# Offsetting weight tiles and activation tiles of a decoder layer by 0, 16, 32 or 48 bytes within 64

## The chip, the cores and the metric

The kernel runs on one core of a Trainium2 chip. The metric is the device time of one execution in microseconds (us). Of the kernel before, three runs gave 895.13, 894.33 and 894.97 us; the median is 894.97 us. A difference of under 0.2% of that (1.8 us) counts as no change here.

## The reference, cut to what matters

One layer of a hybrid decoder on 512 tokens of 1024 features, in float32. What is left out here are the insides of the three branches.

```python
h = _rmsnorm(x, g_mix)
proj = h @ w_in                      # 1024 x 7424: RG-LRU input and gate, q/k/v, memory q, three branch gates
y_lru, y_dil, y_mem = ...            # RG-LRU scan, dilated attention, memory attention; each @ its own output weight
merged = sum_b sigmoid(gates_b + b_gate_b) * y_b
x = x + merged @ w_out               # 1024 x 1024
hm = _rmsnorm(x, g_mlp)
x = x + jnp.square(jax.nn.relu(hm @ w_mlp_in)) @ w_mlp_out    # 1024 x 4096, 4096 x 1024
return _rmsnorm(x, g_final)
```

## The kernel before, in words

Every large product is made of three: a float32 operand is split into a high part in a shortened float32 form (`whi`, `hT_hi`, `ah`) and the exact remainder in the same form (`wlo`, `hT_lo`, `al`), and the kernel adds high by high, high by low and low by high in PSUM.

Weights come in slabs of 1 MB from DRAM into two `raw` buffers. `split_w` (line 162) makes from each half of a slab a tile `whi` (ScalarE, a copy) and a tile `wlo` (VectorE, a subtraction), both 128 x 1024 numbers, that is 4096 bytes in each partition. Each of the two names has four buffers used in turn.

A matmul on TensorE has a stationary operand, loaded into the array by a weight load (PEld in the profile), and a moving operand that streams through the array column by column. While one matmul streams, the weight load of the next one runs. Two forms matter:

- `mm3` (line 187, matmuls at lines 191 to 193), used for the input projection, the branch outputs and the first MLP product. The weight tile is stationary, the activations move: `hT` (normalised x, transposed), `hmT` (the same for the MLP), `y`, `odh`/`odl`, `omh`/`oml` (branch results) with 512 columns, `mT` (memory) with 256. A weight tile serves 24 matmuls in a row. `half_proj` (lines 247 to 251) does the same in halves of 256 columns.
- `out_step` (line 932, matmuls at lines 936 to 938), used for the output projection and the second MLP product. Here the activations are stationary and the weight tile moves with 512 columns (256 in the last token tile). The activations are `mrg` (eight merged tiles), `ah`/`al` (the first three of eight tiles of each quarter of the MLP) and `act` (the other five). `mrg` and `act` share ten buffers of 4096 bytes. `v_proj` (lines 513 to 515) also lets the weights move, with 256 columns.

The MLP runs in four quarters: `mlp_in(q+1)` is issued ahead of `mlp_out(q)`. The order of all engines' instructions comes out of the tile framework, which also gives every tile its address and every instruction its waits. Its pools place tiles at multiples of 32 bytes. In the built program the tiles of this story lie at these addresses modulo 64 bytes:

| tiles | before | after |
|---|---|---|
| `hT`, `hmT`, `y`, `odh`, `odl`, `omh`, `oml`, `ah`, `al` | 32 | 32 |
| `mT`, LRU inputs and gate weights, memory-attention tiles | 0 | 0 |
| `whi`, four buffers in turn | 32, 32, 32, 32 | 32, 48, 32, 48 |
| `wlo`, four buffers in turn | 32, 32, 32, 32 | 32, 16, 32, 16 |
| `mrg` and `act` in the shared buffers | 0 | 0, 0, 16, 48 and again |
| the fourth of eight activation tiles of a quarter | 0 | 32 |

Every slice that a matmul takes of these tiles begins a multiple of 512 bytes into its tile, so the address modulo 64 is that of the tile. What the text calls the relation of a pair is the address of the stationary operand that is being loaded minus the address of the operand that moves meanwhile, modulo 64. Counted over the built programs, pairs in the shortened float32 form:

| relation | 512 columns, before | after | 256 columns, before | after |
|---|---|---|---|---|
| 0 (equal) | 2516 | 1399 | 529 | 295 |
| 32 apart | 726 | 258 | 125 | 56 |
| 16 | 0 | 963 | 0 | 142 |
| 48 | 0 | 622 | 0 | 161 |

Of the kernel before, what the change touches and what calls it, by code (L numbers as in the profile page):

```python
# [12 lines left out]
F32R = mybir.dt.float32r  # L13
# [4 lines left out]
P = 128  # L18
# [34 lines left out]
def _bucket_onehots():  # L53
    """[33, 3, 384]: column m of group g picks the bias row at its offset; row 32 marks masked offsets."""
    oh = np.zeros((NUM_BUCKETS + 1, 3, 384), np.float32)
    m = np.arange(384)
    for g in range(3):
        if g == 0:
            off = 255 - m
            valid = (off >= 0) & (off <= 128)  # L60
            dist = off
        elif g == 1:
            off = 127 - m
            valid = off >= 0
            dist = 4 * off
        else:
            off = 127 - m
            valid = (off >= 0) & (off % 4 == 0)
            dist = 4 * off
        b = _bucket(np.maximum(dist, 0))  # L70
        for j in m:
            oh[b[j] if valid[j] else NUM_BUCKETS, g, j] = 1.0
    return oh


def _head_select():
    """[4, 2, 128]: column p of pair hp picks head 2*hp + p // 64."""
    s = np.zeros((HPG, 2, P), np.float32)
    for hp in range(2):
        for p in range(P):  # L80
            s[2 * hp + p // HD, hp, p] = 1.0
    return s


class _Engine:
    """An engine whose instructions can be pinned to program order."""

# [15 lines left out]
class _Interleave:  # L103
    """Program order: dense matmul groups advance a clock; side generators yield the delay (in us of
    tensor-engine work) that their next step should stay behind."""

# [33 lines left out]
def hybrid_block(ctx: ExitStack, tc: tile.TileContext, x, mem, g_mix, w_in, b_gate, conv_w, conv_b,  # L140
# [19 lines left out]

# [1 line left out]
    def split_w(src, n1, n2, lo_eng=None):  # L162
        hi = wp.tile([P, n1, n2], F32R, name="whi", tag="whi", bufs=4)
        A.activation(hi, src, AF.Copy)
        lo = wp.tile([P, n1, n2], F32R, name="wlo", tag="wlo", bufs=4)
        (lo_eng or V).tensor_sub(lo, src, f(hi))
        return hi, lo
# [8 lines left out]
    def slab(parts):  # L176
        """parts: (weight, first column) of 128 columns each; yields the split halves one by one."""
        raw = raw_tile(KT, 256)
        if parts[0][0] is parts[1][0] and parts[0][1] + P == parts[1][1]:
            nc.sync.dma_start(raw, cols(parts[0][0], parts[0][1], 256))  # L180
        else:
            for i, (w, c0) in enumerate(parts):
                nc.sync.dma_start(raw[:, :, i * P:(i + 1) * P], cols(w, c0, P))
        return [split_w(raw[:, :, i * P:(i + 1) * P], KT, P) for i in range(len(parts))]

    def mm3(ps, w, act, nk, k0=0, us=0.648):
        """ps = w.T @ act over nk row blocks, w = (hi, lo) stationary, act(k) -> (hi, lo) moving."""
        whi, wlo = w
        for k in range(nk):
            ah, al = act(k)  # L190
            PE.matmul(ps, whi[:, k0 + k, :], ah, start=k == 0, stop=False)  # L191
            PE.matmul(ps, whi[:, k0 + k, :], al, start=False, stop=False)  # L192
            PE.matmul(ps, wlo[:, k0 + k, :], ah, start=False, stop=k == nk - 1)  # L193
            if k % 2 == 1 and k < nk - 1:
                sch.tick(2 * us)
        # the caller ticks the rest after its evacuation

# [1 line left out]
    ident = cst.tile([P, P], F32, name="ident")  # L199
# [7 lines left out]
    def rstd(xt, sq, tag):  # L207
        """sq: scratch as wide as xt; returns [P, 1] rsqrt(mean(x^2) + eps)."""
        ss = sm.tile([P, 1], F32, name="ss", tag="ss" + tag, bufs=2)
        A.activation(sq, xt, AF.Square, accum_out=ss)  # L210
        return rstd_of(ss, tag)
# [12 lines left out]
    def transp(hn, dst, t):  # L224
        """hn [tokens, D] of token tile t, transposed and split into dst = (hi, lo)."""
        for half in range(2):
# [12 lines left out]
    def half_proj(items, act, evac, mid):  # L239
        """items: split stationaries; two token halves, the second after mid() was emitted."""  # L240
        pss = [psum() for _ in items]
# [14 lines left out]

# [1 line left out]
    xr = x.rearrange("o (t p) d -> p (o t) d", p=P)  # L258
# [16 lines left out]
    nc.sync.dma_start(first_raw[:, :, P:256], cols(w_in, O_GELU, P))  # L275
    # the tensor engine's clock gate opens while the first tokens are on their way
    warm = psum()
# [17 lines left out]

    # per-feature vectors, one column per 128 features
    vrow = st.tile([72, P], F32, name="vrow")
# [14 lines left out]

# [1 line left out]
    ylru = {}  # L314
# [31 lines left out]
    def lru_gate(c, xc, xh, xlo, rg_hi, rg_lo):  # L346
# [11 lines left out]
        V.scalar_tensor_tensor(xc, ti, 1.0, xc, op0=ALU.add, op1=ALU.mult)  # L358
        # t = tanh(-log(a) / 2) = (1 - a) / (1 + a); 1 / (1 + t) starts from (1 + a) / 2
        rc = t512("rc", 1)  # L360
# [21 lines left out]
    def start_rest():  # L382
        """the other two token tiles, the constants, then what the first LRU chunk needs."""
        for t in (2, 3):
            transp(hns[t], hT, t)

    def small_consts():
# [5 lines left out]
        for g in range(3):  # L393
            ps = psum()
            PE.matmul(ps[0:HPG, 0:384], rb[:, g * HPG:(g + 1) * HPG], oh[:, g, :], start=True, stop=True)
            V.tensor_copy(bvec[:, g, :], ps[0:HPG, 0:384])
        # Toeplitz bias tiles: 128 copies of each vector, read back with a row pitch one short
        n_ = HPG * 3 * 384
# [14 lines left out]

    # softplus(-lam) = max(-lam, 0) + log1p(exp(-|lam|)), log1p(e) = 2 atanh(e / (2 + e))
    sp2 = cst.tile([P, NC_LRU], F32, name="sp2")
# [50 lines left out]
    softplus()  # L466
    # block-diagonal recurrence gates, two 64-blocks per 128 features
    rg_raw = raw_tile(2 * NC_LRU, P)
# [8 lines left out]
    V.tensor_sub(rg_lo, rg_raw, f(rg_hi))  # L477
# [1 line left out]
    def q2k(name, dt=F32):  # L479
        return big.tile([P, S], dt, name=name, tag="q", bufs=12)  # L480

    def qk_proj(g, nm):
        """two chunks (heads 0-1, 2-3) of q (scaled) or k; groups 1, 2 in residue order (t mod 4, t // 4)."""
        o = (O_Q if nm == "q" else O_K) + g * 256
# [15 lines left out]
    def v_proj(g):  # L500
        """[128 tokens, 4 token tiles, 256]; token tile = block for group 0, residue for groups 1, 2,
        which are brought to residue order on their way through DRAM."""
        vt = big.tile([P, 4, 256], F32, name="vt", tag="V", bufs=4)
# [24 lines left out]

    # memory tokens, normalised here and transposed once there is room
    mr = mem.rearrange("o (t p) d -> p (o t) d", p=P)  # L530
# [31 lines left out]

# [1 line left out]
    mT = (ap_.tile([P, KT, N_MEM], F32R, name="mT_hi", tag="mT_hi"),  # L564
# [7 lines left out]

# [1 line left out]
    def softmax_stats(sc, mz, i):  # L574
        """sc [P, 4 heads, n]: exp(s - max) in place; mz[:, 0|1, i, :] = max, sum."""
        V.tensor_reduce(mz[:, 0, i, :], sc, axis=AX.X, op=ALU.max)
# [10 lines left out]
    def p_T(groups):  # L587
        """groups of 4 [128, 128] slices, transposed; returns SBUF tiles [128 keys, 4, 128 queries]."""
        res = []
# [31 lines left out]
    def av_out(dst, view, terms):  # L621
        """terms: (transposed P [keys, 4, queries], V [keys, 256]) summed into [128, 2 head pairs, 128]."""
        ps = psum()
# [37 lines left out]
    def stats_T(mz, permute):  # L661
        """mz [P tokens, 2, 4 tiles, 4 heads] -> [4 heads, 2, 512 tokens] in token order."""
        st_ = pr_tile([HPG, 2, S], "stT")
# [14 lines left out]
    def side_b():  # L678
# [4 lines left out]
        for r in range(4):  # L683
# [7 lines left out]
            yield 1.0  # L691
        # merge by the softmax denominators
        sA = stats_T(mzA, False)
# [47 lines left out]

# [1 line left out]
    km = []  # L743
# [38 lines left out]

# [1 line left out]
    omem = {}  # L784
# [59 lines left out]

# [1 line left out]
    branches = (ylru, odil, omem)  # L846
# [63 lines left out]
    def act_tile(name):  # L910
        return ep.tile([P, 2, S], F32R, name=name, tag="act", bufs=10)

# [4 lines left out]

# [1 line left out]
    x2 = {}  # L919
# [48 lines left out]

# [1 line left out]
    def hmmov(k):  # L970
        return hmT[0][:, k, :], hmT[1][:, k, :]

    def mlp_evac(act, ps):
# [5 lines left out]
        else:  # L979
            t_ = act_tile("act")  # L980
            ah, al = t_[:, 0], t_[:, 1]
# [95 lines left out]
```

## Time and profile before

| | |
|---|---|
| median of three runs | 894.97 us |
| span of the profiled execution, first to last instruction | 892.8 us |
| TensorE matmul / weight load busy | 879.6 us / 734.8 us |
| VectorE / ScalarE / GpSimd busy | 451.6 / 356.7 / 26.0 us |
| matmul records | 4383 |
| DMA, mean over the span | 106 GB/s |

The profiled execution is one execution, and its own time is known by its span: 892.8 us, 2.2 us under the median of the runs; these 2.2 us lie outside the first and the last instruction. A matmul's record is longer than the distance to the next matmul's start, since matmuls overlap: what one costs in a dense stretch is the distance from start to start, read from the timeline.

### The profile page before, as it was taken

Reading aid. Unit: us, or ns where it says so; the run is one execution under the profiler, and the core shown is the slowest. Engines: PE = TensorE matmul, PEld = TensorE weight load, DVE = VectorE, ACT = ScalarE, POOL = GpSimd, SP = SyncE. Lnnn points to the kernel's source line nnn. Section 1 sums busy time; section 2 is a strip of 40 time slices with the busy share of each in tenths; the row PEclk is TensorE's granted clock in tenths of the full one; section 3 lists DMA queues with packets and bytes.
Section 4 is the critical chain, followed back from the end, with each engine's and each line's share of the span. In section 5 each row is a group of like instructions: output and inputs, shape, how many; then the busy total and the mean of one; then the engine's idle time right before and its main releaser. Section 6 shows DMA issues by size and latency. Waiting matters only on the chain.

```text
span 892.8 us, 10656 instructions
## 1 busy us (share of the span) xinstructions
PE 879.6 (99%) x4383; PEld 734.8 (82%) x4383; DVE 451.6 (51%) x628; ACT 356.7 (40%) x565; POOL 26.0 (3%) x34
## 2 busy tenths in 40 slices
PE   8999999999999999999999999999999999999997
PEld 7788888889888888888888888888888888888886
DVE  5778666764678543343424365444334433443342
ACT  5457666654644532332323154433113311441122
POOL 3110000000000000000000000000000000000020
PEclk9899999999999999999999999999999999999999
DMA  7673333333421222332434214322333323332202
GB/s 239 186 227 95 95 95 95 95 111 127 140 85 60 70 96 71 118 97 81 130 133 160 83 46 144 95 94 96 94 96 97 106 90 97 111 105 93 98 6 94
DMA packets 79164, 94.87 MB, mean 106 GB/s; under 512 B 3611, under 2 KB 64103, under 8 KB 78988
## 3 DMA queue, kind: packets, MB, share of 16 engines
q1 hardware_dynamic: 77916, 88.15, 31.6%
q0 software_dynamic: 1056, 5.52, 1.9%
q8 instruction: 34, 0.56, 0.3%
q10 hardware_dynamic: 144, 0.52, 0.1%
q14 instruction: 14, 0.11, 0.0%
HBM read 91.03 MB, written 5.52 MB: 108 GB/s over the span
## 4 chain that ended last, share of the span: by engine, by line
PE 92%; DVE 2%; DMA 2%; ACT 1%; issue 1%; POOL 0%; SPq 0%; POOLq 0%; ACTq 0%; DVEq 0%
PE ps L191 19%; PE ps L192 19%; PE ps L193 18%; PE ps L938 8%; PE ps L936 8%; PE ps L937 8%; PE ps L513 1%; PE ps L515 1%; PE ps L514 1%; DMA x<-in_x_dram 1%; PE ps L248 1%; PE ps L626 1%; PE ps L247 1%; PE ps L593 1%; PE ps L251 1%
## 5 line engine op out<-in xcount | busy, mean ns | idle before, releaser
L95 DVE TENSOR_TENSOR wlo<-raw,whi 128x1024 fp32r<-128x1024 f32 (+1 forms) x153 | 182.9, 1199 | 314.2 <-ACT whi L95 309.7
L95 ACT ACTIVATE whi<-raw 128x1024 fp32r<-128x1024 f32 (+1 forms) x154 | 159.5, 1037 | 394.2 <-PE ps L192 223.0
L191 PE MATMUL ps<-hT_hi,whi 128*128 128x512 f32 x400 | 156.6, 392 | 0.0
L193 PE MATMUL ps<-hT_hi,wlo 128*128 128x512 f32 x400 | 155.9, 390 | 0.0
L192 PE MATMUL ps<-hT_lo,whi 128*128 128x512 f32 x400 | 155.9, 390 | 0.0
L192 PE MATMUL ps<-hmT_lo,whi 128*128 128x512 f32 x240 | 93.4, 389 | 0.0
L193 PE MATMUL ps<-hmT_hi,wlo 128*128 128x512 f32 x240 | 93.4, 389 | 0.0
L191 PE MATMUL ps<-hmT_hi,whi 128*128 128x512 f32 x240 | 93.2, 389 | 0.0
L191 PEld LDWEIGHTS ps<-hT_hi,whi 128*128 128x128 f32 x400 | 75.1, 188 | 16.4 <-issue 0.6
L193 PEld LDWEIGHTS ps<-hT_hi,wlo 128*128 128x128 f32 x400 | 75.1, 188 | 15.8
L192 PEld LDWEIGHTS ps<-hT_lo,whi 128*128 128x128 f32 x400 | 75.1, 188 | 15.2
L938 PE MATMUL ps<-whi,act 128*128 128x512 f32 (+1 forms) x165 | 64.1, 389 | 0.0
L937 PE MATMUL ps<-wlo,act 128*128 128x512 f32 (+1 forms) x165 | 64.1, 388 | 0.0
L936 PE MATMUL ps<-whi,act 128*128 128x512 f32 (+1 forms) x165 | 64.1, 388 | 0.0
L192 PEld LDWEIGHTS ps<-hmT_lo,whi 128*128 128x128 f32 x240 | 45.1, 188 | 9.3
L191 PEld LDWEIGHTS ps<-hmT_hi,whi 128*128 128x128 f32 x240 | 45.0, 188 | 9.4
L193 PEld LDWEIGHTS ps<-hmT_hi,wlo 128*128 128x128 f32 x240 | 45.1, 188 | 9.3
L95 DVE TENSOR_TENSOR x<-x,ps 128x512 f32<-128x512 f32 (+1 forms) x41 | 27.7, 675 | 24.9 <-PE ps L938 24.6
L938 PE MATMUL ps<-whi,al 128*128 128x512 f32 (+1 forms) x99 | 38.0, 384 | 0.0
L937 PE MATMUL ps<-wlo,ah 128*128 128x512 f32 (+1 forms) x99 | 37.9, 383 | 0.0
L936 PE MATMUL ps<-whi,ah 128*128 128x512 f32 (+1 forms) x99 | 37.9, 383 | 0.0
L937 PEld LDWEIGHTS ps<-wlo,act 128*128 128x128 f32 x165 | 31.0, 188 | 7.1
(253 smaller groups left out, 1355.6 us busy)
## 6 DMA issues: line engine op xcount, KB each, us to landing
raw<-in_w_in_dram SPq DMA_DIRECT2D x23, 1024.0 KB
raw<-in_w_mlp_in_dram SPq DMA_DIRECT2D x16, 1024.0 KB
raw<-in_w_mlp_out_dram SPq DMA_DIRECT2D x16, 1024.0 KB
raw<-in_w_in_dram SPq DMA_DIRECT2D x12, 512.0 KB
raw<-in_w_mem_kv_dram SPq DMA_DIRECT2D x4, 1024.0 KB
raw<-in_w_out_dram SPq DMA_DIRECT2D x4, 1024.0 KB
x<-in_x_dram SPq DMA_DIRECT2D x7, 512.0 KB
raw<-in_w_lru_out_dram SPq DMA_DIRECT2D x4, 768.0 KB
```

The lines of the kernel that those rows point to most:

```text
L95: r = fn(*a, **k)
L191: PE.matmul(ps, whi[:, k0 + k, :], ah, start=k == 0, stop=False)
L192: PE.matmul(ps, whi[:, k0 + k, :], al, start=False, stop=False)
L193: PE.matmul(ps, wlo[:, k0 + k, :], ah, start=False, stop=k == nk - 1)
L247: PE.matmul(ps[:, sl], whi[:, k, :], ah, start=k == 0, stop=False)
L248: PE.matmul(ps[:, sl], whi[:, k, :], al, start=False, stop=False)
L251: PE.matmul(ps[:, sl], wlo[:, k, :], act[0][:, k, sl], start=False, stop=k == KT - 1)
L513: PE.matmul(ps[:, 0:256], ah, hi[:, k % 4, :], start=k == 0, stop=False)
L514: PE.matmul(ps[:, 0:256], ah, lo[:, k % 4, :], start=False, stop=False)
L936: PE.matmul(ps, ah[:, sl], hi[:, k % 2, :], start=k == 0, stop=False)
L937: PE.matmul(ps, ah[:, sl], lo[:, k % 2, :], start=False, stop=False)
L938: PE.matmul(ps, al[:, sl], hi[:, k % 2, :], start=False, stop=k == KT - 1)
```

## The change

The tile pools get new names for the same buffers. Instead of four buffers under one name, `whi` and `wlo` have one buffer under each of four names, used in the same turn; every other one is 16 bytes longer, and the data begins 16 bytes into it. The framework rounds the longer tiles up to 32 bytes, so that the tiles behind them move by 32. The shared activation buffers get the same treatment with four names of two buffers: eight in place of ten. Since a quarter of the MLP needs five and two quarters live at once, the fourth of its eight activation tiles goes to a buffer of another name (`y4`, of which four hold `x2` and two are free by then). Comments and docstrings go too.

```diff
+    turn = {"w": 0, "act": 0}
+
+    def shifted(pool, name, n1, n2, j, bufs):
+
+        o = 4 * (j % 2)
+        t = pool.tile([P, 1024 + o], F32R, name=name, tag=f"{name}{j}", bufs=bufs)
+        return t[:, o:o + n1 * n2].rearrange("p (a b) -> p a b", a=n1)
+
     def split_w(src, n1, n2, lo_eng=None):
-        hi = wp.tile([P, n1, n2], F32R, name="whi", tag="whi", bufs=4)
+        j = turn["w"] % 4
+        turn["w"] += 1
+        hi = shifted(wp, "whi", n1, n2, j, 1)
         A.activation(hi, src, AF.Copy)
-        lo = wp.tile([P, n1, n2], F32R, name="wlo", tag="wlo", bufs=4)
+        lo = shifted(wp, "wlo", n1, n2, j, 1)
         (lo_eng or V).tensor_sub(lo, src, f(hi))
         return hi, lo
...
     def act_tile(name):
-        return ep.tile([P, 2, S], F32R, name=name, tag="act", bufs=10)
+        turn["act"] += 1
+        return shifted(ep, "act", 2, S, turn["act"] % 4, 2)
...
         if i < 3:
             ah, al = q2k("ah", F32R), q2k("al", F32R)
         else:
-            t_ = act_tile("act")
+            t_ = act_tile("act") if i > 3 else big.tile([P, 2, S], F32R, name="act3", tag="y4", bufs=6)
             ah, al = t_[:, 0], t_[:, 1]
```

No instruction is added, removed or moved: on each of the five engines the built program of the changed kernel has the same instructions with the same shapes in the same order, and with the same waits but for one. The load of `gbmlp` (line 237, in the output projection's lead) waits in addition for an earlier DMA of GpSimd's queue, because its buffer now overlaps one that this DMA used.

## Rows read from the trace of the kernel before

**Rows 1.** The page: busy times, granted clock by slices, the chain by engine

```profile
span 892.8 us, 10656 instructions
...
PE 879.6 (99%) x4383; PEld 734.8 (82%) x4383; DVE 451.6 (51%) x628; ACT 356.7 (40%) x565; POOL 26.0 (3%) x34
...
PEclk9899999999999999999999999999999999999999
...
PE 92%; DVE 2%; DMA 2%; ACT 1%; issue 1%; POOL 0%; SPq 0%; POOLq 0%; ACTq 0%; DVEq 0%
```

**Rows 2.** Timeline of TensorE (start us, length us), 55 matmuls of `mm3`, relation equal

```profile
127.69 0.39 PE L193 MATMUL ps<-hT_hi,wlo 128*128 128x512 f32 x1
127.92 0.39 PE L191 MATMUL ps<-hT_hi,whi 128*128 128x512 f32 x1
...
139.93 0.39 PE L193 MATMUL ps<-hT_hi,wlo 128*128 128x512 f32 x1
```

**Rows 3.** Timeline of TensorE, 36 matmuls of `out_step`, relation 32 apart

```profile
631.76 0.40 PE L936 MATMUL ps<-whi,act 128*128 128x512 f32 x1
...
639.93 0.40 PE L938 MATMUL ps<-whi,act 128*128 128x512 f32 x1
```

**Rows 4.** Timeline of TensorE, 77 matmuls of `v_proj`, 256 columns, relation equal

```profile
81.83 0.28 PE L515 MATMUL ps<-whi,hT_lo 128*128 128x256 f32 x1
...
90.94 0.28 PE L513 MATMUL ps<-whi,hT_hi 128*128 128x256 f32 x1
```

**Rows 5.** Timeline of TensorE, 11 matmuls on `mT`, 256 columns, relation 32 apart

```profile
210.93 0.28 PE L192 MATMUL ps<-mT_lo,whi 128*128 128x256 f32 x1
...
212.11 0.28 PE L193 MATMUL ps<-mT_hi,wlo 128*128 128x256 f32 x1
```

**Rows 6.** Timeline of TensorE, LRU gates after `mm3`: equal relation, another place

```profile
119.69 0.40 PE L350 MATMUL ps<-xh,rg_hi 128*128 128x512 f32 x1
119.92 0.40 PE L351 MATMUL ps<-xlo,rg_hi 128*128 128x512 f32 x1
120.16 0.40 PE L352 MATMUL ps<-xh,rg_lo 128*128 128x512 f32 x1
120.39 0.39 PE L350 MATMUL ps<-xh,rg_hi 128*128 128x512 f32 x1
120.62 0.39 PE L351 MATMUL ps<-xlo,rg_hi 128*128 128x512 f32 x1
120.85 0.39 PE L352 MATMUL ps<-xh,rg_lo 128*128 128x512 f32 x1
```

**Rows 7.** Groups of TensorE (busy us, mean ns | idle), shapes kept apart

```profile
L191 PE MATMUL ps<-hT_hi,whi 128*128 128x512 f32 x400 | 156.6, 392 | 0.0
L192 PE MATMUL ps<-hmT_lo,whi 128*128 128x512 f32 x240 | 93.4, 389 | 0.0
L937 PE MATMUL ps<-wlo,act 128*128 128x512 f32 x155 | 61.3, 395 | 0.0
L937 PE MATMUL ps<-wlo,ah 128*128 128x512 f32 x93 | 36.2, 389 | 0.0
```

**Rows 8.** Stretches of Rows 2 and 3: PE busy, granted clock, DMA share

```profile
128.00:130.00 2.00, 2.00 (x11) 1.00 0.00 0
632.00:634.00 2.00, 2.00 (x10) 1.00 0.00 0
```

**Rows 9.** Groups of VectorE and ScalarE that write the split weights

```profile
L95 DVE TENSOR_TENSOR wlo<-raw,whi 128x1024 fp32r<-128x1024 f32 (+1 forms) x153 | 182.9, 1199 | 314.2 <-ACT whi L95 309.7 <-issue 4.4
L95 ACT ACTIVATE whi<-raw 128x1024 fp32r<-128x1024 f32 (+1 forms) x154 | 159.5, 1037 | 394.2 <-PE ps L192 223.0 <-PE ps L938 107.6 <-DVE x L95 27.2
```

**Rows 10.** The load of `gbmlp` on SyncE's queue (ns min/median/max, first and last start)

```profile
L237 SPq DMA_DIRECT2D gbmlp<-in_g_mlp_dram x1: 341/341/341, 320.6 to 320.6; - x1
```

## The prediction

> **What bounds the kernel now.** I read the page first. TensorE is busy 99% of a span of 892.8 us and holds 92% of the chain that ended last; VectorE is at 51%, ScalarE at 40% [rows 1]. So only what makes TensorE's matmuls come quicker or slower changes the time, or a wait long enough to stop it. The granted clock is full in nearly every slice [rows 1] and 1.00 in both stretches that I compare below, with no DMA traffic in either [rows 8]: the 2.4 GHz level, and nothing to win or lose there as long as TensorE stays as dense.
>
> Since the change moves addresses only, the second view is the timeline of TensorE, where the reader is to take distances from start to start. Four dense stretches stand in the rows, and they differ in width and in the relation of the pair (the weight being loaded against the operand that streams):
>
> - 512 columns, equal: 127.69 to 139.93 us in 54 steps, 226.7 ns each [rows 2].
> - 512 columns, 32 apart: 631.76 to 639.93 us in 35 steps, 233.4 ns each [rows 3].
> - 256 columns, equal: 81.83 to 90.94 us in 76 steps, 119.9 ns each [rows 4].
> - 256 columns, 32 apart: 210.93 to 212.11 us in 10 steps, 118.0 ns each [rows 5].
>
> The same instruction at the same clock thus costs 6.7 ns more or 1.9 ns less when the two tiles lie 32 bytes apart. The groups show it again without any choice of a stretch: the mean length of a record is 389 ns for 240 matmuls with an equal relation and for the 93 on `ah`, and 395 for the 155 on `act` in the same loop [rows 7]. The two widths with equal relation differ by 106.8 ns for 256 columns, 0.417 ns a column; so 512 columns are 213.6 ns and each matmul pays a further 13.1 ns (equal) or 19.8 ns (32 apart). With 256 columns the further part is 13.1 and 11.2 ns. This further part, 3,242 and 654 times, is what the addresses can move.
>
> It is not settled at once. Where the LRU gates come in between, with an equal relation too but other tiles, six matmuls take from 119.69 to 120.85 us, 232 ns a step, with steps from 0.23 to 0.24 us [rows 6], before the stretch comes to the 226.7 of rows 2. A change of tiles costs a start-up: five steps at 232 in place of 226.7 are 27 ns.
>
> Here a rule of the Trainium skill speaks against the change. TensorE: Matmul & The Clock Gate (Part 2, Step-by-step) gives TensorE two independent read ports, one for the moving operand and one for the weight load, and SBUF — State Buffer (SBUF: two separate sides) says that TensorE never waits on anyone there. By that rule the relation of the two could not matter, and the time would stay at that of the second rival below. The trace does not bear it out, since 226.7 and 233.4 ns stand for the same instruction. The same page's section Back-to-back issue gap has 2.5 ns beyond the columns at full clock, with which 512 columns would be 215.8 ns; as an estimate from that page all 1,585 wide pairs with a new relation would then save some 11 to 18 ns each.
>
> **The change part by part.** Instructions: none is added or moved, so nothing is charged for issue, DMA or evacuation. The order is the same on all engines.
>
> Weights, wide matmuls: 1,585 of 3,242 pairs get a relation of 16 or 48, which no dense stretch of before has. Of equal ones 1,117 are lost and of those 32 apart 468. With u for the new spacing the change is 1,117 x (u - 226.7) + 468 x (u - 233.4) ns. Bounds: below, the further part goes to nothing, u = 213.6; above, the dearest step in the rows, 240 at its rounding [rows 6], or as a mean 236. Between them I need a value. The only move that rows price, 32 bytes, changed the further part by 6.7 ns with 512 columns and 1.9 ns with 256, in opposite directions, 4.3 ns on average. I take that size, downwards from the equal relation: u = 222.4. Downwards, because with an equal relation the two streams touch the same places of each 64 bytes, and the one cheaper row is of an unequal relation [rows 5]; this is the weakest step. It gives 1,117 x -4.3 = -4.8 us and 468 x -11.0 = -5.1 us.
>
> Narrow matmuls: 303 pairs get the new relation, 234 of them from equal (-4.3 ns each, -1.0 us) and 69 from 32 apart (-2.4 ns, to 115.6; -0.2 us).
>
> Start-ups: under `mm3` a weight tile serves 24 matmuls, and its neighbours now have another relation. 2,208 wide matmuls there make some 92 tiles, each with a start-up of 27 ns that rows 2 don't have: +2.5 us. The bounds are 0, if no state is lost at a change of tile, and 92 x 24 x 5.3 ns = 11.7 us, if a tile never settles.
>
> Writers of the tiles: `wlo` on VectorE takes 1,199 ns and `whi` on ScalarE 1,037 ns for 1,024 columns; ahead of these groups the engines sat idle for 314.2 and 394.2 us [rows 9]. An offset of 16 bytes in what they write has no row. Were it dearer by a tenth, 16 to 18 us on engines idle some twenty times as long would be covered; were it cheaper, TensorE would not notice. I cost it at nothing. Without that cover the tenth would stand in full.
>
> Buffers: eight shared activation buffers in place of ten, and one from `y4`, give each quarter its five again, two quarters deep; a tile waits for the same matmuls as before. The added wait stands ahead of the `gbmlp` load, which starts at 320.6 us [rows 10]; behind it on SyncE's queue are the weight slabs for the gates. It is for a DMA that read or wrote the small start-up tiles early in the program, long landed by then. Zero; if it did hold the queue, a slab late by 1 us stops TensorE for at most that.
>
> Sum against the profiled execution: -4.8 - 5.1 - 1.0 - 0.2 + 2.5 = -8.6 us, so a span of 884.2 us; with 2.2 us outside the span 886.4 us, against the median of 894.97.
>
> **The rivals.**
>
> The new relation is worse than the equal one. All matmuls with another relation than equal that are 512 wide cost more in these rows: 233.4 settled, 232 in start-up. If 16 and 48 behave as a start-up that never ends, u = 232: 1,117 x 5.3 - 468 x 1.4 = +5.3 us; start-ups remain only in the 46 unshifted tiles (+1.2 us), narrow ones cost nothing. That is +6.5 us, 901.5 us; at u = 236 it is 10.4 + 1.2 + 1.2 = +12.8, 907.8. It decides from u = 227 upwards: with 92 start-ups the sum is zero at about that spacing. For it: most pairs start from the cheapest wide relation known. Against: the narrow row.
>
> The grain is coarser than 16 bytes, or the pairs average out: 1,117 keep 226.7 and 468 keep 233.4, and no new start-up follows. 895 us, to within 2 us. For it: two kinds of tile with equal relation, at 32 and at 0 modulo 64, show the same kind of steps, so absolute place does not seem to matter; and the change could as well be too fine to be seen. Against: 32 bytes are seen clearly.
>
> The conflict goes altogether: u = 213.6. Then 1,117 x -13.1 - 468 x 19.8 = -23.9 us, narrow -3.8 us, start-ups only in the 46 unshifted tiles, +1.2: 868.5 us. For it: odd multiples of 16 might never meet the other stream. Against: no step of the start-up comes under 0.23 us [rows 6], though it passes through several positions.
>
> **How the numbers follow.** Forecast, a smaller further part, 0.42 (spacings from 218 to 225, 877 to 891 us); no conflict at all 0.06; no matter 0.11; worse 0.41. A change of 0.2%, 1.8 us, is about what can be told from none. Of the forecast nearly all and of the last rival all lie on the faster side; some of the worse ones end within 1.8 us. Faster 0.48, same 0.12, slower 0.40. The range for 8 in 10 leaves out most of the no-conflict case and the dearest of the worse one: 874 to 904. The likeliest case's own is 877 to 891.
>
> **What would show it.** In the timeline after, the stretches of `mm3` should alternate every 24 matmuls: 226.7 ns for a tile at 32, about 222 for one at 48 and 16. The group on `act` should have a mean record of under 390 ns in place of 395. The forecast is wrong if the shifted tiles show 227 or more; the start-up term is wrong if a tile at 32 settles at once. If VectorE's `wlo` grew much over 1,199 ns with TensorE idle behind it, the address cost would lie with the writers.

## The result, and the profile after

The changed kernel takes 903.94 us (median of 4 runs, 901.64 to 904.71) and the kernel before 894.65 us (4 runs, 893.55 to 895.13): a ratio of 1.0101, 95% interval 1.0086 to 1.0116. It is slower by 1%; the forecast was 886.4 us, faster by 1%.

The page after, to be laid beside [rows 1]:

```profile
span 902.7 us, 10656 instructions
...
PE 888.6 (98%) x4383; PEld 736.5 (82%) x4383; DVE 452.1 (50%) x628; ACT 356.7 (40%) x565; POOL 26.1 (3%) x34
...
PEclk9899999999999999999999999999999999999999
...
PE 92%; DVE 2%; ACT 2%; issue 1%; DMA 1%; POOL 0%; POOLq 0%; ACTq 0%; DVEq 0%
```

The span grew by 9.9 us and TensorE's busy time by 9.0, with the same instructions. No new wait and no other engine has come into the chain; the matmuls themselves take longer. The granted clock shows the same digits, but a 9 stands for all from 0.90 up, and shorter stretches differ. In the memory attention the profiled run of the changed kernel stood at the half level, 1.2 GHz, where the kernel before was at full clock (stretch in us, PE, PEld, VectorE, ScalarE and GpSimd busy, granted clock, DMA); the changed kernel comes second:

```profile
275.50:276.50 1.00, 1.00 (x10) 1.00 (x9) 1.00 (x3) 0.35 (x1) 0.00 (x0) 1.00 0.00 0
```

```profile
278.50:280.50 2.00, 2.00 (x12) 2.00 (x11) 2.00 (x4) 0.31 (x1) 0.00 (x0) 0.50 0.00 0
```

Ahead of it, from 274.5 to 276.2 us, stand eight matmuls on 4 partitions each, as they do at this place in the kernel before, whose clock stayed full. The 16 matmuls from 277.6 to 281.2 us took 1.5 us more than the same ones before, most of it from this clock. Of the six slower kernels on record three have such a stretch here in their profiled run (this one, the weights alone and the first scan below) and three have none and are slower all the same. The groups of the changed kernel that answer to [rows 7] and [rows 9] (busy us, mean ns of one | idle before):

```profile
L201 PE MATMUL ps<-hT_hi,whi 128*128 128x512 f32 x400 | 158.2, 395 | 0.0
L202 PE MATMUL ps<-hmT_lo,whi 128*128 128x512 f32 x240 | 94.5, 394 | 0.0
L948 PE MATMUL ps<-wlo,act 128*128 128x512 f32 x219 | 86.1, 393 | 0.0
L948 PE MATMUL ps<-wlo,ah 128*128 128x512 f32 x93 | 36.4, 391 | 0.0
...
L95 DVE TENSOR_TENSOR wlo<-raw,whi 128x1024 fp32r<-128x1024 f32 (+1 forms) x153 | 182.9, 1199 | 319.3 <-ACT whi L95 315.1 <-issue 4.2
...
L95 ACT ACTIVATE whi<-raw 128x1024 fp32r<-128x1024 f32 (+1 forms) x154 | 159.5, 1037 | 401.4 <-PE ps L202 231.1 <-PE ps L949 107.6 <-DVE x L95 26.9
```

Matmuls on `hT` and `hmT`, which ran at 392 and 389 ns a record, are now at 395 and 394. Those on `act` gained only 2 ns (the group now holds `mrg` too, which ran at 395 before), those on `ah` lost 2. The writers of the tiles take the same time to the nanosecond.

One turn of the four weights in the timeline of the changed kernel (start us, length us): the first and the last of 24 matmuls under each weight. The third is the weight whose tiles stayed in place; the fourth is the first with an offset; the first two are those behind it in memory.

```profile
585.60 0.39 PE L201 MATMUL ps<-hmT_hi,whi 128*128 128x512 f32 x1
...
590.96 0.39 PE L203 MATMUL ps<-hmT_hi,wlo 128*128 128x512 f32 x1
591.19 0.39 PE L201 MATMUL ps<-hmT_hi,whi 128*128 128x512 f32 x1
...
596.48 0.40 PE L203 MATMUL ps<-hmT_hi,wlo 128*128 128x512 f32 x1
596.71 0.39 PE L201 MATMUL ps<-hmT_hi,whi 128*128 128x512 f32 x1
...
601.94 0.39 PE L203 MATMUL ps<-hmT_hi,wlo 128*128 128x512 f32 x1
602.17 0.39 PE L201 MATMUL ps<-hmT_hi,whi 128*128 128x512 f32 x1
...
607.52 0.39 PE L203 MATMUL ps<-hmT_hi,wlo 128*128 128x512 f32 x1
```

Divided by 23 steps these are 233.0, 230.0, 227.4 and 232.6 ns (by the trace's nanoseconds 233.1, 229.9, 227.2 and 233.0); before, all four ran at 226.7 [rows 2]. Only the untouched weight comes back to 226.7, after three steps. The mean of the four is 230.8; 4.1 ns more for some 2,208 matmuls under `mm3` are 9.1 us, nearly the whole loss. Step by step the 9.9 us of the two spans are 8.6 for the matmuls of 512 columns under `mm3` from 45 us on at full clock, 1.5 in the stretch at half clock and 0.9 before 45 us, less 0.7 for the matmuls of 256 columns and 0.4 for `out_step`.

The surprise is the first tile, at 233.1. It has no offset of its own. The two longer tiles ahead of it in memory, one `whi` and one `wlo`, each rounded up by 32 bytes, push it by 64, and the table ahead of the prediction, which counts modulo 64, calls it equal.

### The profile page after: what moved, and what is told of

Read it like the earlier page. It is cut to its first block, busy times and chain, and to the rows that moved or that the text cites. A ratio compares the mean times of both kernels' runs of the same rounds, so it can differ in the third digit from the quotient of the medians.

```text
span 902.7 us, 10656 instructions
## 1 busy us (share of the span) xinstructions
PE 888.6 (98%) x4383; PEld 736.5 (82%) x4383; DVE 452.1 (50%) x628; ACT 356.7 (40%) x565; POOL 26.1 (3%) x34
## 4 chain that ended last, share of the span: by engine, by line
PE 92%; DVE 2%; ACT 2%; issue 1%; DMA 1%; POOL 0%; POOLq 0%; ACTq 0%; DVEq 0%
PE ps L201 19%; PE ps L202 19%; PE ps L203 19%; PE ps L947 8%; PE ps L949 8%; PE ps L948 8%; PE ps L523 1%; PE ps L525 1%; PE ps L524 1%; PE ps L258 1%; PE ps L636 1%; PE ps L257 1%; PE ps L603 1%; PE ps L261 1%; DMA rb<-in_rel_bias_dram 1%
## 5 line engine op out<-in xcount | busy, mean ns | idle before, releaser
L95 DVE TENSOR_TENSOR wlo<-raw,whi 128x1024 fp32r<-128x1024 f32 (+1 forms) x153 | 182.9, 1199 | 319.3 <-ACT whi L95 315.1
L95 ACT ACTIVATE whi<-raw 128x1024 fp32r<-128x1024 f32 (+1 forms) x154 | 159.5, 1037 | 401.4 <-PE ps L202 231.1
L947 PE MATMUL ps<-whi,act 128*128 128x512 f32 (+1 forms) x229 | 89.3, 390 | 0.0
L948 PE MATMUL ps<-wlo,act 128*128 128x512 f32 (+1 forms) x229 | 88.9, 388 | 0.0
L949 PE MATMUL ps<-whi,act 128*128 128x512 f32 (+1 forms) x229 | 88.8, 388 | 0.0
L949 PEld LDWEIGHTS ps<-whi,act 128*128 128x128 f32 x229 | 43.0, 188 | 9.7
L948 PEld LDWEIGHTS ps<-wlo,act 128*128 128x128 f32 x229 | 43.0, 188 | 9.4
L947 PEld LDWEIGHTS ps<-whi,act 128*128 128x128 f32 x229 | 43.0, 188 | 9.4
```

Source lines behind the costliest of these rows:

```text
L95: r = fn(*a, **k)
L947: PE.matmul(ps, ah[:, sl], hi[:, k % 2, :], start=k == 0, stop=False)
L948: PE.matmul(ps, ah[:, sl], lo[:, k % 2, :], start=False, stop=False)
L949: PE.matmul(ps, al[:, sl], hi[:, k % 2, :], start=False, stop=k == KT - 1)
```

## The experiments

Three theories stood first. B: the new names, buffers and the added wait cost the time. R: each pair pays by its own relation modulo 64. S: with offsets that alternate the pace never settles. Distances below are weight minus `hT` (or activation) in bytes.

**The names alone.** All of the change, with every offset zero.

```diff
-        o = 4 * (j % 2)
+        o = 0
```

> The change with every offset at 0: the new buffer names, eight activation buffers in place of ten and the one tile in y4, but all weights at 32 modulo 64. Theory S (unsettled pace: what costs is that TensorE's pace, once disturbed by a tile at another address, stays in dearer cycles, equal pairs included): 895 us, no change. Rival R (each pair pays by its own relation alone, 232 ns at 16 and 48, 226.7 when equal): 895 us. Rival B (the buffers or the added wait cost the time): 899 to 904 us.

892.91 us against 894.76; ratio 0.998 (0.997 to 0.999). B falls: nothing is lost to buffers or the wait. The small gain fits in part with the one activation tile in `y4`, which lies equal to its weights: 93 matmuls of 512 columns at 6.7 ns are 0.6 us, as the trace has it; the rest was not pursued.

**The weights alone.** Kernel before, with the change's new `split_w`; the activation tiles stay.

```diff
-        hi = wp.tile([P, n1, n2], F32R, name="whi", tag="whi", bufs=4)
+        hi = shifted(wp, "whi", n1, n2, j, 1)
...
-        lo = wp.tile([P, n1, n2], F32R, name="wlo", tag="wlo", bufs=4)
+        lo = shifted(wp, "wlo", n1, n2, j, 1)
```

> Weights offset as in the change, activation buffers as before. S: mm3 pays all of its +9 us, 903 to 905 us, and equal tiles show about 232 ns. R: the 1,094 shifted mm3 pairs cost 5.3 ns each, +5.8 us, 900 to 901 us, and equal tiles stay at 226.7 ns. B: 895 us.

903.49 us; ratio 1.0096 (1.0079 to 1.0114). The whole loss is here, more than the 900 to 901 us of R.

**The activation tiles alone.** The change with the two lines above undone.

```diff
-        hi = shifted(wp, "whi", n1, n2, j, 1)
+        hi = wp.tile([P, n1, n2], F32R, name="whi", tag="whi", bufs=4)
...
-        lo = shifted(wp, "wlo", n1, n2, j, 1)
+        lo = wp.tile([P, n1, n2], F32R, name="wlo", tag="wlo", bufs=4)
```

> Activation buffers offset as in the change, weights as before. S and R alike: mm3 as before; in out_step the pairs that were 32 apart go from 233.4 to about 231 ns where they get 16 or 48, some 300 of them, -0.7 us: 894 us. B: 899 to 904 us.

893.53 us; ratio 0.9988 (0.9977 to 1.0). No loss; the gain that the forecast gave to these pairs isn't there beyond that of the names.

**One tile in four with an offset.** As the weights alone, but only the second of the four is offset, so three of four keep their relation modulo 64.

```diff
-        o = 4 * (j % 2)
+        o = 4 if j == 1 else 0
```

> Only one weight tile in four is offset (48 and 16), the three after it are at 32. R: a quarter of the mm3 pairs pays 5.3 ns, +2.9 us: 898 us, equal tiles at 226.7 ns. My forecast's start-up of five steps: 0.6 us on top, 898.5 us. S, if a disturbed pace persists: the three equal tiles after the shifted one stay near 233 ns for up to 72 matmuls, up to +10 us more: 903 to 908 us.

904.33 us; ratio 1.0108 (1.009 to 1.0125): as slow as with two offset. By its time alone this was S. The timeline says otherwise; the last weight of a turn, not offset and 64 bytes away, and the first of the next, untouched:

```profile
610.61 0.39 PE L200 MATMUL ps<-hmT_hi,whi 128*128 128x512 f32 x1
...
615.98 0.40 PE L202 MATMUL ps<-hmT_hi,wlo 128*128 128x512 f32 x1
616.21 0.39 PE L200 MATMUL ps<-hmT_hi,whi 128*128 128x512 f32 x1
...
621.44 0.39 PE L202 MATMUL ps<-hmT_hi,wlo 128*128 128x512 f32 x1
```

233.5 and 227.4 ns. The pace does settle in each tile, at a value that goes with the tile: the two that lie 64 away at 233.2 ns to the end. R and S both fail, and theory M took their place: the distance counts modulo 128.

**A scan from 0 to 48 bytes.** The weights are cut out of one large tile, so that high and low part lie alike.

```diff
+    wall = wp.tile([P, 8 * 1024 + 12 + 0], F32R, name="whi")
...
-        hi = wp.tile([P, n1, n2], F32R, name="whi", tag="whi", bufs=4)
+        o = 2048 * j + 4 * j + 0
+        hi = wall[:, o:o + n1 * n2].rearrange("p (a b) -> p a b", a=n1)
...
-        lo = wp.tile([P, n1, n2], F32R, name="wlo", tag="wlo", bufs=4)
+        lo = wall[:, o + 1024:o + 1024 + n1 * n2].rearrange("p (a b) -> p a b", a=n1)
```

> Kernel: the weight tiles are cut out of one large tile so that high and low part of a weight lie alike, and the four weights in turn lie 0, 16, 32 and 48 bytes from the operand hT, counted within 128. Theory M (the pace of a 512-column matmul hangs on the distance between weight tile and moving tile within 128 bytes, and comes to rest inside each tile of 24 matmuls): the tiles at 0 run at 226.7 ns as in the kernel before, those at 32 at 233.3 ns as its out_step does (that one is 32 apart), those at 16 and 48 each at a pace of its own between 226 and 237 ns, the same in every such tile. Three quarters of the weights leave the distance 0, so the time is 899 to 910 us. Theory S (once weights of several offsets alternate, the pace stays unsettled): every tile averages about 232.5 ns whatever its distance, 904 us. Theory R (distance within 64): here it cannot be told from M.

903.54 us; ratio 1.0101 (1.0086 to 1.0117).

**A scan from 64 to 112 bytes.** The same with 16 elements more.

```diff
-        o = 2048 * j + 4 * j + 0
+        o = 2048 * j + 4 * j + 16
```

> Kernel: as the scan of 0 to 48 bytes, with the four weights in turn 64, 80, 96 and 112 bytes from hT. Theory M: the tiles at 64 run at 233.3 ns, as those 64 apart in the changed kernel; those at 80, 96 and 112 each at a pace of its own, and the one at 96 the same as the one at 32 only if the effect is symmetric; none needs to be at 226.7 ns, and the time is 902 to 912 us. Theory R (distance within 64): the tiles at 64 run at 226.7 ns like those at 0, the one at 96 at 233.3 like 32, the others like 16 and 48, and the time equals that of the scan of 0 to 48 bytes within 0.3%. Theory S: about 232.5 ns in all, 904 us.

908.73 us; ratio 1.0161 (1.0147 to 1.0175). The two scans differ, so modulo 64 is out. The table has the mean spacing of the 24 matmuls in the 16 to 18 undisturbed tiles at each distance (13 at 0 and at 64), start to start, and the mean of the settled last third:

| distance | 0 | 16 | 32 | 48 | 64 | 80 | 96 | 112 |
|---|---|---|---|---|---|---|---|---|
| mean, ns | 227.5 | 233.3 or 226.7 | 233.1 | 233.3 | 233.3 | 231.7 | 234.0 | 233.2 |
| settled, ns | 226.7 | 233.4 or 226.7 | 233.3 | 233.3 | 233.3 | 232.0 | 234.0 | 233.3 |

No distance is under 226.7. At 16 there are two paces, and each tile has one of them throughout. In the first scan, 24 matmuls at 16 bytes early in the program, and 24 later:

```profile
145.81 0.40 PE L197 MATMUL ps<-hT_hi,whi 128*128 128x512 f32 x1
...
151.18 0.39 PE L199 MATMUL ps<-hT_hi,whi 128*128 128x512 f32 x1
```

```profile
600.24 0.39 PE L197 MATMUL ps<-hmT_hi,whi 128*128 128x512 f32 x1
...
605.45 0.40 PE L199 MATMUL ps<-hmT_hi,whi 128*128 128x512 f32 x1
```

233.5 and 226.5 ns at the same distance, against M, which had one pace in every such tile. The later one comes straight behind a tile at 0 that has settled. Ahead of the early one stand six matmuls at 0 that follow on those of the LRU gates and are still in their start-up (144.42 to 145.81 us, 232 ns a step). So what came before does matter at this one distance, as S has it for all; whether this is the condition was not tried.

**merged and act moved by 32 bytes.** From 32 apart to 64.

```diff
+    pad = ep.tile([P, 8], F32, name="pad")
+    V.memset(pad, 0.0)
```

> Kernel: the weights stay as before; only the tiles of merged and act move by 32 bytes, so that out_step and the second product's deep half go from 32 apart to 0 apart within 64, which is 64 apart within 128. Theory R (within 64): these some 650 matmuls go from 233.4 to 226.7 ns, 4.4 us less, 890.5 us. Theory M (within 128): 64 apart costs 233.3 ns like 32 apart; no gain, 894 to 896 us. Theory S says nothing other than R here, since all tiles of one name lie alike.

894.79 us; ratio 1.0004 (0.9995 to 1.0013): no gain, as M has it and R does not.

**merged and act moved by 96 bytes.** From 32 apart to 0 within 128.

```diff
+    pad = ep.tile([P, 24], F32, name="pad")
+    V.memset(pad, 0.0)
```

> Kernel: the weights stay as before; only the tiles of merged and act move by 96 bytes, so that out_step and the second product's deep half lie 0 apart within 128 from their weights. Theory M: these some 650 matmuls go from 233.4 to 226.7 ns, 4.4 us less: 890.5 us, ratio 0.995. Theory R gives the same 890.5 here, but also for the shift by 32 bytes. If only the weights' changes matter and not the distance, nothing moves: 895 us.

893.25 us; ratio 0.9993 (0.9985 to 1.0002). The 4.4 us that M promised did not come, and `out_step` in this kernel's timeline, two stages of 24 on `mrg`, shows why:

```profile
506.95 0.39 PE L938 MATMUL ps<-whi,mrg 128*128 128x512 f32 x1
...
517.88 0.40 PE L940 MATMUL ps<-whi,mrg 128*128 128x512 f32 x1
```

47 steps of 232.6 ns; before, they were 233.4 [rows 3]. M falls too: 0 within 128 is not enough. The tiles now lay 128 apart within 256. Two theories were left. M2: the period is 256 or 512. P: not the distance counts, but that these tiles lie far up in memory.

**All operands equal within 512.** One tile of 24 bytes goes to a pool that lies lower, so weights, `hT` and the rest move up by 32 bytes against `merged`, `act` and the normalised memory, which stay.

```diff
-        return sm.tile([P, NC_LRU], F32, name=name)
+        return (cst if name == "ng" else sm).tile([P, NC_LRU], F32, name=name)
```

> Kernel: the one before, with one small tile of 24 bytes put in another pool, so that weights, hT and all tiles of the attention move up by 32 bytes together while merged, act and the normalised memory stay; nothing is padded. All operands of the 512-column matmuls then lie 0 apart within 512 bytes. Shifting merged and act to 0 within 128 (which is 128 within 512) left them at 232.4 ns, so theory M as first put (128) is refuted. Theory M2 (the pace hangs on the distance within 256 or 512): the some 700 matmuls with merged or act now go to 226.7 ns, 4 to 5 us less, 889 to 891 us, ratio 0.995. Theory P (what counts is where merged and act lie, far up in memory, not the distance): they stay at 232 to 233 ns, 894 us. If an absolute address within 64 counted for the weights, the tiles with hT would leave 226.7 ns; under M2 they stay.

888.78 us against 894.32; ratio 0.9942 (0.993 to 0.9954), faster than both kernels. The same stage of `out_step`, and the groups that answer to [rows 7]:

```profile
504.60 0.39 PE L936 MATMUL ps<-whi,mrg 128*128 128x512 f32 x1
...
515.25 0.40 PE L938 MATMUL ps<-whi,mrg 128*128 128x512 f32 x1
```

```profile
L191 PE MATMUL ps<-hT_hi,whi 128*128 128x512 f32 x400 | 156.8, 392 | 0.0
L192 PE MATMUL ps<-hmT_lo,whi 128*128 128x512 f32 x240 | 93.4, 389 | 0.0
L937 PE MATMUL ps<-wlo,act 128*128 128x512 f32 x155 | 60.3, 389 | 0.0
L937 PE MATMUL ps<-wlo,ah 128*128 128x512 f32 x93 | 36.2, 389 | 0.0
```

47 steps of 226.6 ns, and `act` at 389 in place of 395: P falls, since these tiles did not move. `hT` and `hmT` keep their pace though they moved by 32 bytes, so no absolute address within 64 bytes shows. Step by step the 657 matmuls with a partner in both traces give 4.2 us. The profiled span is 6.4 us shorter; 1.8 of the rest lie in the 256-column matmuls outside these loops, where from 30 to 40 us the granted clock was 1.00 against 0.95 in the profiled run before; this part isn't claimed for the addresses.

The same run shows matmuls of 256 columns change the other way. Those on `mT` went from 32 apart to equal; the 14 steps of their settled stretch, to be laid beside [rows 5]:

```profile
209.85 0.28 PE L191 MATMUL ps<-mT_hi,whi 128*128 128x256 f32 x1
...
211.53 0.28 PE L193 MATMUL ps<-mT_hi,wlo 128*128 128x256 f32 x1
```

These are 120.0 ns each, close to the 119.9 of equal pairs in [rows 4]; 32 apart it was 118.0. Over the 86 undisturbed ones the mean rose from 117.8 to 119.5 ns.

**A scan of 0, 128, 256 and 384 bytes.** As the first scan; six tiny tiles and `nsp` go to the pool of the LRU stage to make room.

```diff
-        o = 2048 * j + 4 * j + 0
+        o = 2048 * j + 32 * j
...
-        return sm.tile([P, NC_LRU], F32, name=name)
+        return lpool["p"].tile([P, NC_LRU], F32, name=name)
```

> Kernel: the four weights in turn lie 0, 128, 256 and 384 bytes from hT (high and low part alike; a few tiny tiles are in another pool to make room; merged and act are 288 apart). Theory M2, read from the tiles of 24 matmuls: those at 0 at 226.7 ns; those at 128 at 232 to 233 ns as merged and act 128 apart were; if the period is 256, those at 256 at 226.7 ns and those at 384 like 128, about 902 us in all; if it is 512, the ones at 256 and 384 are at 230 to 235 ns too, about 905 us. Theory M as first put (128): all four at 226.7 ns and no loss, 894 us. Theory P: the weights do not lie far up, so all four at 226.7 ns, 894 us.

902.69 us; ratio 1.0093 (1.0073 to 1.0113). One turn, at 128, 256, 384 and 0:

```profile
598.27 0.40 PE L197 MATMUL ps<-hmT_hi,whi 128*128 128x512 f32 x1
...
603.63 0.40 PE L199 MATMUL ps<-hmT_hi,whi 128*128 128x512 f32 x1
603.86 0.39 PE L197 MATMUL ps<-hmT_hi,whi 128*128 128x512 f32 x1
...
609.09 0.40 PE L199 MATMUL ps<-hmT_hi,whi 128*128 128x512 f32 x1
609.32 0.40 PE L197 MATMUL ps<-hmT_hi,whi 128*128 128x512 f32 x1
...
614.67 0.40 PE L199 MATMUL ps<-hmT_hi,whi 128*128 128x512 f32 x1
614.91 0.39 PE L197 MATMUL ps<-hmT_hi,whi 128*128 128x512 f32 x1
...
620.13 0.40 PE L199 MATMUL ps<-hmT_hi,whi 128*128 128x512 f32 x1
```

By nanoseconds 232.7, 227.2, 232.7 and 227.2. Tiles at 256 settle at 226.7 like those at 0, those at 384 like those at 128. So the period is 256 bytes, as far as these two pairs of distances show it.

## Why the prediction was wrong

**What bounds the kernel.** Right in the main: the change of time is TensorE's, and the addresses set its pace in stretches at full clock. But the clock, where the prediction saw "nothing to win or lose", was not the same in the profiled runs. Of the 9.9 us between their spans, 1.5 lie in the stretch around 278.5 to 280.5 us that stood at 0.50, and 0.9 before 45 us, where the clock from 30 to 40 us was 0.90 against 0.95.

**The relation.** The step "Weights, wide matmuls: 1,585 of 3,242 pairs get a relation of 16 or 48" failed, and with it the table that it counts from. It took 64 as the period, on no row; the kernel before has only two distances, and they cannot tell 64 from 256. In the changed kernel a quarter of the weight tiles lie 64 away, not 0, and settle at 233.3 ns where the sum left them at 226.7 ns. That is about 552 of the 2,208 matmuls by 6.4 ns, 3.5 us that stood in no term; in the traces the 532 with a partner lost 3.4 us.

**Downwards.** "I take that size, downwards from the equal relation: u = 222.4" had the wrong sign, and it was the step that the prediction called its weakest. Measured: 233.0 ns for tiles at 16 and 48, 229.9 for those at 80 and 112 (both counted as 16 and 48 before), 4.9 us more on the 1,093 matmuls under `mm3` with a partner in both traces. The forecast had -4.8 us for what had been equal. The argument from the one cheaper row [rows 5] was of 256 columns, where it holds, and did not carry over to 512.

**The act pairs.** -5.1 us was put on 468 pairs that were 32 apart, with u 11.0 ns lower. By the program 398 of them got 16 or 48 and 70 became equal modulo 64. The 394 undisturbed ones of the first ran at 231.2 ns instead of 233.2, worth 0.8 us, and matmuls on `ah` and `al`, which had been equal, lost 0.8. The test that the prediction set, a mean record on `act` under 390 ns, gave 393.

**Start-ups.** Charged with 27 ns for each of 92 tiles. The size was right and the number not: 563 matched matmuls in tiles at 0, some 23 tiles, took 0.66 us more, 28 ns a tile. The other three quarters do not come back to 226.7 at all, so for them there is no such term, and 0.7 us stands in place of 2.5.

**Narrow matmuls.** Forecast -1.2 us. The direction was right and the size about half. From 45 us on, without the stretch at half clock, the matmuls of 256 columns took 0.7 us less. Of the undisturbed ones, the 251 with a new relation took 1.4 ns less each; 202 more, whose relation modulo 64 stayed but whose distance modulo 256 changed and to which the forecast gave nothing, took 1.6 ns less. So with 256 columns the equal distance is the dearer one; what failed was to carry that sign over to 512.

**Writers, buffers, the added wait.** Right: 1,199 and 1,037 ns as before, and the names alone cost nothing.

**The rivals.** "The new relation is worse than the equal one" is what came. Its price, 901.5 us at u = 232, lacked the tiles at 64, and so 903.94 lies above it; its reason (a start-up that never ends) was not the right one, since the paces are settled and each goes with a distance. The rule of the Trainium skill (TensorE: Matmul & The Clock Gate, Part 2, Step-by-step) of two independent read ports, by which distance should not matter, does not agree with these runs: under `mm3` 226.7 ns at 0 and 256, 230 to 234 at all others tried but 16.

What stays open: why the period is 256 bytes, what holds a tile at 16 bytes on the one or the other pace, and distances that aren't a multiple of 16. None of these was tried.

## What to carry to other kernels

Where TensorE is the bound with float32r matmuls of 512 columns, look up where the weight tiles and the operands that stream past them lie, and give both the same address modulo 256; moving one tile of 24 bytes was worth 0.6% here. With 256 columns the same address was the dearer case, by some 2 ns, so look first which width the time is in. A padded tile shifts all tiles behind it in its pool, so count the real addresses and not the offsets. Two distances in one trace don't give the period of an effect: a scan in one run, with one distance per tile of 24 matmuls, does.

## What was not expected of the hardware

- The spacing of 512-column matmuls hangs on the distance of weight and moving operand modulo 256 bytes: 226.7 ns at 0 and 256, 232.4 at 128 and 384, 233.3 at 32, 48, 64 and 112, 232.0 at 80, 234.0 at 96.
- At 16 bytes two paces last through a tile, 226.7 and 233.4 ns, and a settled tile at 0 directly ahead goes with the faster one.
- Behind a tile at another distance a tile at 0 is at its pace after three steps in most cases and after eight in some (the changed kernel: three at 596.71 us, eight at 685.37 us).
- Where the high part lies at 80 and the low part at 112, the pace is 229.9 ns, under the 231.7 and 233.2 that both parts at 80 or both at 112 give: a mix can't be had from the table.
- With 256 columns the order is turned round: 120.0 ns settled at 0, and for 44 matmuls on `hmT` that the change put from 0 to 64, 115.8 in place of 120.3.
